# Two-layer S5 and gated DeltaNet step: Toeplitz products of the state space stage split into high and low parts

## The chip, the cores and the metric

The kernel runs on one core of one Trainium2 chip. The metric is the device time of one execution in microseconds (us), as the median of the runs. A core has five engines that run side by side and wait for each other by semaphores: TensorE (PE, matrix products), VectorE (DVE), ScalarE (ACT), GpSimd (POOL) and SyncE (SP, which only issues DMAs here). In this kernel products are written to tiles in PSUM, the other tiles lie in SBUF.

## The reference

Layer 0 is a diagonal complex state space mixer (S5), layer 1 a gated delta rule; both get 2048 prompt tokens and 8 samples of 16 tokens. Cut to what matters here:

```python
def s5_scan(u, h_re, h_im, ar, ai, bbr, bbi, c_re, c_im):
    # per position: x_t = Abar x_{t-1} + Bbar u_t, y_t = Re(C x_t); 64 groups, 16 channels, 64 states each
    ...

def s5_branch(h, ...):
    u, z = split(h @ w_in)
    y, hr, hi = s5_scan(u, ...)
    y = gelu(y + d * u)
    y = y * sigmoid(y @ w_glu + b_glu)
    y = y * silu(z)
    return y @ w_out, hr, hi
```

All arithmetic is float32.

## The kernel before

The program goes through stages: the S5 input products (to about 270 us of the profile), the state space stage (about 270 to 600 us), the gate and output products of layer 0, then layer 1. The change lies in the state space stage.

The tokens are cut into chunks of 8 (NCH = 272 chunks, 256 of them of the prompt). Within a chunk the recurrence is written as a Toeplitz matrix: the part of y that comes from the same chunk is one product of `toe` (128x128, 8 positions by 16 channels, from the impulse response with `d` on its diagonal) with `u` (128 x 272). What comes from earlier chunks goes over the states: `pb` is the chunk's contribution to the state (products of `ab` and `u`), VectorE rotates it by the tables `tw` (f, then z), scans along the chunks (`tensor_tensor_scan`), rotates back (t, then xs), and a product with `ca` adds it to y.

The stage has 16 blocks of 4 groups. `s5_setup(b)` makes `ab`, `ca` and the Toeplitz matrix of block b: the impulse response `kp` goes to DRAM (`k_d`) and comes back as `toe` in four DMAs. `s5_load(b)` loads u and tw. `s5_main(b)` does the block. The loop calls load and setup of block b+1 ahead of the main part of block b.

In most of its products the kernel writes a value as the sum of a high and a low part in the type `F32R`, and the product as three: high x high, high x low, low x high. A product of `F32R` stands as one record in the profile (one pass). `split_w` makes the parts: ScalarE casts the high part, VectorE (or the engine in `lo_eng`) subtracts for the low part. Before, `ca` and `xs` are split so, and `toe` x `u` is a float32 product.

Pools give each tile a number of buffers: b1 has one of each tag, b2 two. A tile's buffer is free when its readers are done. `ps_b` has one buffer for pb, `ps_y` two for py.

`z_block` is work of another kind: the z half of the input projection (tiles pdz, 64 blocks of 24 one-pass products of 128x272). Nothing in the stage waits for it. 58 of the blocks may run at any time, and fill PE; the last six are held until the last y products of the stage (`later([ends...])`).

What sets the order of instructions in this stage is a scheduler that works at build time with its own idea of durations; each engine then runs its list in order, and so a change of a few instructions moves the z products and others among them. When the stage is done, `ps5.close()` frees the SBUF of its pools, and the gate weights (wgr) are loaded there.

Of the kernel before, what the change touches and what calls it, by code (L numbers as in the profile page):

```python
# [11 lines left out]
F32R = mybir.dt.float32r  # L12
# [6 lines left out]
P = 128  # L19
# [3 lines left out]
NCH = 272  # L23
# [18 lines left out]
def bc(ap, axis, n):  # L42
    a = ap.unsqueeze(axis)
    shape = list(a.shape)
    shape[axis] = n
    return a.broadcast_to(shape)


def dram_ap(t, offset, dims):
    return bass.AP(t.tensor, t.offset + offset, [list(d) for d in dims])  # L50
# [3 lines left out]
def kernel(ctx: ExitStack, tc: tile.TileContext, I, O, upto="Z"):  # L54
    nc = tc.nc
# [18 lines left out]
    T, V, S, G, SY = (Engine(e) for e in (nc.tensor, nc.vector, nc.scalar, nc.gpsimd, nc.sync))  # L74
# [54 lines left out]
    def split_w(dst_hi, dst_lo, raw, lo_eng=None):  # L129
        S.copy(dst_hi, raw)  # L130
        (lo_eng or V).tensor_sub(dst_lo, raw, dst_hi.bitcast(F32))
# [102 lines left out]
    with ExitStack() as pa:  # L234
# [333 lines left out]
        for j in range(8):  # L568
            hh, hl = hcur
# [62 lines left out]
    with ExitStack() as pb:  # L632
        ps5 = pb.enter_context(ExitStack())
        b2 = ps5.enter_context(tc.tile_pool(reuse_waits="tile", name="b2", bufs=2))
        b1 = ps5.enter_context(tc.tile_pool(reuse_waits="tile", name="b1", bufs=1))
# [25 lines left out]
        def s5_setup(b):  # L661
            sp = b3.tile([P, SPW], F32, tag="sp", bufs=2, name=f"sp_{b}")
            nc.sync.dma_start(sp, sp_d[b])
            pw = sp[:, PWO:BBO].rearrange("p (l r n) -> p l r n", l=2, r=3)
            bbv = sp[:, BBO:BDO].rearrange("p (r l c) -> p r l c", r=2, l=2)
            bdv = sp[:, BDO:CCO].rearrange("p (r l m) -> p r l m", r=2, l=2)
            ccv = sp[:, CCO:SPW].rearrange("p (r l c) -> p r l c", r=2, l=2)

            abt = b1.tile([P, 2, 2, 8, 16], F32, tag="abt", name=f"abt{b}")
            tt = b1.tile([P, 2, 2, 9, 16], F32, tag="tt", name=f"abtt{b}")  # L670
            for l in range(2):
                V.tensor_mul(abt[:, l], bc(bc(bbv[:, 0, l], 1, 8), 1, 2), bc(pw[:, l, 0:2, 0:8], 3, 16))
                V.tensor_mul(tt[:, l, :, 0:8], bc(bc(bbv[:, 1, l], 1, 8), 1, 2), bc(pw[:, l, 1:3, 0:8], 3, 16))
            V.tensor_add(abt.rearrange("p l r n c -> p (l r) (n c)"), abt.rearrange("p l r n c -> p (l r) (n c)"),
                         tt.rearrange("p l r n c -> p (l r) (n c)")[:, :, 0:128])
            ab = b2.tile([P, 4, P], F32, tag="ab", name=f"ab{b}")
            pt = ps_t.tile([P, 4, P], F32, tag="t", name=f"abT{b}")
            for q in range(4):
                T.transpose(pt[:, q, :], abt[:, q // 2, q % 2].rearrange("p n c -> p (n c)"), ident)
            S.copy(ab, pt)  # L680

            ca = b3.tile([P, 2, 2, 9, 16], F32, tag="ca", bufs=2, name=f"ca{b}")
            t2 = b1.tile([P, 2, 2, 9, 16], F32, tag="tt", name=f"cat{b}")
            for l in range(2):
                V.tensor_mul(ca[:, l], bc(bc(ccv[:, 0, l], 1, 9), 1, 2), bc(pw[:, l, 1:3], 3, 16))
                V.tensor_mul(t2[:, l], bc(bc(ccv[:, 1, l], 1, 9), 1, 2), bc(pw[:, l, 0:2], 3, 16))
            V.tensor_sub(ca, ca, t2)
            cs_ = [b2.tile([P, 2, 2, P], F32R, tag="ca" + i, name=f"ca{i}{b}") for i in "hl"]
            split_w(*(t.rearrange("p l r (n c) -> p (l r) n c", c=16) for t in cs_),
                    ca[:, :, :, 1:9].rearrange("p l r n c -> p (l r) n c"))  # L690

            pk = ps_t.tile([P, P], F32, tag="t", name=f"pk{b}")
            for l in range(2):
                for r in range(2):
                    T.matmul(pk[32 * l:32 * l + 32, :], lhsT=bdv[:, r, l],
                             rhs=ca[:, l, r, 0:8, :].rearrange("p n c -> p (n c)"), start=(r == 0), stop=(r == 1),
                             tile_position=(0, 32 * l))
            kp = b2.tile([64, 240], F32, tag="kp", bufs=1, name=f"kp{b}")
            G.memset(kp[:, 0:112], 0.0)
            S.copy(kp[:, 112:240], pk[0:64])  # L700
            V.scalar_tensor_tensor(kp[:, 112:128], dmask, d16[:, b:b + 1], kp[:, 112:128], op0=ALU.mult, op1=ALU.add)
            nc.scalar.dma_start(k_d[b], kp)
            toe = b2.tile([P, 4, P], F32, tag="toe", name=f"toe{b}")
            for g in range(4):
                nc.sync.dma_start(toe[:, g, :], dram_ap(k_d[b], 16 * g * 240, [[16, 8], [240, 16], [1, P]]))
            return cs_, ab, toe

        def s5_load(b):
            u = b2.tile([P, 4, NCH], F32, tag="ur", name=f"u{b}")
# [6 lines left out]
        def s5_main(b, u, tw, ca, ab, toe):  # L716
            prs = slice(2 * b, 2 * b + 2)
            z = b2.tile([P, 2, 2, NPC], F32, tag="z", name="z")
            x = b2.tile([P, 2, 2, NCH], F32, tag="x", name=f"xs{b}")
            xh = x[:, :, :, NPC:NCH].rearrange("p l r (q h) -> p l r q h", h=2)  # L720
            G.memset(x[:, :, :, 0:1], 0.0)
# [5 lines left out]
            f = b2.tile([P, 2, 2, 2, NPC], F32, tag="f", name=f"f{b}")  # L727
            for pl in range(2):
                pb_ = ps_b.tile([P, 2, 512], F32, tag="b", name=f"pb{b}_{pl}")
                for ri in range(2):  # L730
                    for g2 in range(2):
                        T.matmul(pb_[64 * g2:64 * g2 + 64, ri, 0:NCH], lhsT=ab[:, 2 * pl + 1 - ri, 64 * g2:64 * g2 + 64],
                                 rhs=u[:, 2 * pl + g2], start=True, stop=True, tile_position=(0, 64 * g2))
# [34 lines left out]
            for pl in range(2):  # L768
                y = b2.tile([P, 2, NCH], F32, tag="y", name=f"y{b}_{pl}")
                pys = [ps_y.tile([P, NCH], F32, tag="y", name=f"py{b}_{2 * pl + i}") for i in range(2)]  # L770
                for i in range(2):
                    T.matmul(pys[i], lhsT=toe[:, 2 * pl + i], rhs=u[:, 2 * pl + i], start=True, stop=False)
                for r in range(2):
                    for wi, xi in ((0, 0), (0, 1), (1, 0)):
                        for i in range(2):
                            ln = slice(64 * i, 64 * i + 64)
                            i_ = T.matmul(pys[i], lhsT=ca[wi][ln, pl, r], rhs=xs[xi][ln, pl, r],
                                          start=False, stop=(r == 1 and wi == 1), tile_position=(64 * i, 0))
                ends.append(i_.ins)
                for i in range(2):  # L780
                    S.activation(y[:, i, :], pys[i], AF.Gelu_apprx_tanh)
                nc.scalar.dma_start(
                    dram_ap(y_d, (b // 2) * 8 * P * NCH + (4 * (b % 2) + 2 * pl) * NCH, [[8 * NCH, P], [1, 2 * NCH]]),
                    y.rearrange("p g c -> p (g c)"))
            return ends

        par = s5_setup(0)
        ld = s5_load(0)
        for b in range(16):
            nxt = (s5_load(b + 1), s5_setup(b + 1)) if b < 15 else None  # L790
            ends = s5_main(b, *ld, *par)
            if nxt:
                ld, par = nxt
# [501 lines left out]
    with pd:  # L1295
# [5 lines left out]
        def hcols(n0, n, s0=0):  # L1301

            g = sum(8 * q.stop <= n0 for q in CG)
            c = slice(n0 // 8 - CG[g].start, (n0 + n) // 8 - CG[g].start)
            return [[slots(h[i], g)[:, s0:, c] for h in hh_] for i in range(2)]
# [37 lines left out]
        for k in range(KC):  # L1343
            sh, xi = modT[:, 24 + k, 0:1], xa[:, k]
# [104 lines left out]
        with ExitStack() as pq:  # L1449
# [51 lines left out]
            for i0, (n0, n) in enumerate(NATT):  # L1501
                ps = psd1.tile([P, 512], F32, tag="d", name=f"pba{n0}")[0:32, 0:n]
                hh, hl = hcols(n0, n)
# [138 lines left out]
        for b in range(4):  # L1642
            rs, cs_ = slice(32 * b, 32 * b + 32), slice(32 * b, 32 * b + 32)
# [437 lines left out]
def _build(arrays, upto="Z"):  # L2081
    import concourse.bacc as bacc

    nc = bacc.Bacc("TRN2", target_bir_lowering=False, num_devices=1)
    I = {k: nc.dram_tensor("in_" + k, v.shape, F32, kind="ExternalInput").ap() for k, v in arrays.items()}
    O = {k: nc.dram_tensor("out_" + k, s, F32, kind="ExternalOutput").ap() for k, s in _OSHAPE.items()}
    with tile.TileContext(nc, schedule_with_timeline_sim=True) as tc:
        dbg = kernel(tc, I, O, upto)
    return nc, dbg
# [9 lines left out]
```

## Time and profile before

| | us |
|---|---|
| median of 3 runs | 2154.48 (2152.29 to 2161.67) |
| profiled execution: span from first to last instruction | 2147.2 |
| median less that span | 7.3 |
| PE busy | 2083.9 (97%) |
| DVE busy | 1558.8 (73%) |
| ACT busy | 980.2 (46%) |
| POOL busy | 473.6 (22%) |
| mean granted TensorE clock | 0.989 |

The profile is of one execution, in which the profiler recorded each instruction's start and end. Its page gives the span alone; the runs were timed apart from it, and the difference of 7.3 us is taken as what lies around a span. Busy time of an engine is the time in which it had an instruction under way; idle time that another engine ended is put down to that one ("<-"). Rows name the line of the kernel, the engine, the operation, the tile written and the tiles read. Each float32 product stands as two records.

### The profile page before, as it was taken

To read this page: it belongs to the slowest core of one execution; us is meant where nothing else is said; L and a number is where in the kernel's file an instruction comes from. 1 tells how busy PE (TensorE), PEld (TensorE's weight loads), DVE (VectorE), ACT (ScalarE), POOL (GpSimd) and SP (SyncE) were. 2 spreads that over 40 slices of the span, in tenths; PEclk is the share of its full clock that TensorE was granted. 3 is DMA by queue.
4 is the path that set the end of the run, shared out by engine and by line. 5 is a ranking of instruction groups with operands and counts; after the bars stand their busy time and mean duration, and the time that the engine had idled before them with its cause. 6 is when DMAs were issued, how large, how long until landed. Compare 5 with 4: busy or idle time off the path is not lost.

```text
span 2147.2 us, 42222 instructions
## 1 busy us (share of the span) xinstructions
PE 2083.9 (97%) x15729; PEld 1851.3 (86%) x15729; DVE 1558.8 (73%) x4017; ACT 980.2 (46%) x2298; POOL 473.6 (22%) x720
## 2 busy tenths in 40 slices
PE   6899999999799999999999999999999899999998
PEld 4888988888599999999888879889987688888887
DVE  6999498999756554446665669688556788888875
ACT  3543433333255544446665422341224556666663
POOL 1267310000112322222100000100011344444430
PEclk9999999999899999999999999999999999999999
DMA  9897744444386533336465313663456844444432
GB/s 278 273 299 234 239 150 149 141 157 148 97 242 220 190 113 110 108 100 218 138 202 171 92 50 86 162 146 103 135 169 217 269 143 126 134 142 147 147 113 70
DMA packets 398666, 344.99 MB, mean 161 GB/s; under 512 B 88410, under 2 KB 359274, under 8 KB 398460
## 3 DMA queue, kind: packets, MB, share of 16 engines
q1 hardware_dynamic: 261388, 234.95, 36.9%
q10 hardware_dynamic: 134256, 99.69, 14.4%
q0 software_dynamic: 2816, 7.65, 1.0%
q8 instruction: 124, 2.03, 0.4%
q14 instruction: 82, 0.67, 0.1%
HBM read 221.40 MB, written 120.80 MB: 159 GB/s over the span
## 4 chain that ended last, share of the span: by engine, by line
PE 86%; DVE 6%; DMA 4%; ACT 2%; issue 1%; SPq 1%; POOL 0%; ACTq 0%; DVEq 0%
PE epo L69 6%; PE pc L150 5%; PE pc L152 5%; PE pc L151 5%; PE pz L152 3%; PE po L150 3%; PE pz L151 3%; PE pdz L151 3%; PE pz L150 3%; PE po L152 3%; PE po L151 3%; PE pdz L150 3%; PE pdz L152 3%; PE pg L152 3%; PE pg L150 3%; PE pg L151 3%
## 5 line engine op out<-in xcount | busy, mean ns | idle before, releaser
L150 PE MATMUL pc<-h1h,wdh 128*128 128x512 f32 (+1 forms) x600 | 216.5, 361 | 0.0
L152 PE MATMUL pc<-h1h,wdl 128*128 128x384 f32 (+1 forms) x600 | 214.9, 358 | 0.0
L151 PE MATMUL pc<-h1l,wdh 128*128 128x384 f32 (+1 forms) x600 | 214.8, 358 | 0.1
L1414 DVE SCALAR_TENSOR_TENSOR ac<-pb,convw,ac 128x384 f32<-128x384 f32 (+3 forms) x288 | 163.6, 591 | 3.3
L150 PE MATMUL pdz<-hhz,wzh 128*128 128x272 f32 x512 | 152.3, 298 | 1.8 <-ACT evz L627 1.8
L151 PE MATMUL pdz<-hlz,wzh 128*128 128x272 f32 x512 | 153.0, 299 | 0.0
L152 PE MATMUL pdz<-hhz,wzl 128*128 128x272 f32 x512 | 151.6, 296 | 0.0
L150 PE MATMUL po<-gh,woh 128*128 128x272 f32 x512 | 148.6, 292 | 2.2 <-ACT gh L942 2.2
L151 PE MATMUL po<-gl,woh 128*128 128x272 f32 x512 | 148.4, 291 | 0.8 <-DVE gl L942 0.8
L152 PE MATMUL po<-gh,wol 128*128 128x272 f32 x512 | 148.7, 292 | 0.0
L151 PE MATMUL pg<-yl,wgh 128*128 128x272 f32 x512 | 148.4, 290 | 0.0
L150 PE MATMUL pg<-yh,wgh 128*128 128x272 f32 x512 | 147.5, 288 | 0.5 <-ACT evz L627 0.5
L152 PE MATMUL pg<-yh,wgl 128*128 128x272 f32 x512 | 147.5, 288 | 0.0
L150 PEld LDWEIGHTS pc<-h1h,wdh 128*128 128x128 f32 x600 | 112.6, 188 | 12.3 <-issue 1.7
L151 PEld LDWEIGHTS pc<-h1l,wdh 128*128 128x128 f32 x600 | 112.7, 188 | 10.4 <-issue 0.8
L152 PEld LDWEIGHTS pc<-h1h,wdl 128*128 128x128 f32 x600 | 112.6, 188 | 10.2 <-issue 0.8
L150 PE MATMUL pd<-hh,wuh 128*128 128x272 f32 x384 | 112.5, 294 | 0.0
L69 PE MATMUL epo<-w2h,ohi 128*128 128x512 f32 x272 | 111.7, 410 | 0.0
L152 PE MATMUL pd<-hh,wul 128*128 128x272 f32 x384 | 110.9, 289 | 0.0
L151 PE MATMUL pd<-hl,wuh 128*128 128x272 f32 x384 | 110.6, 288 | 0.0
L69 PE MATMUL epo<-w2l,ohi 128*128 128x512 f32 x272 | 107.5, 395 | 1.6 <-DMA w2l<-w2l_d 1.5
L939 POOL TENSOR_TENSOR zt<-zt,sz 128x272 f32<-128x272 f32 x64 | 63.4, 996 | 203.5 <-ACT sz L938 194.3
(613 smaller groups left out, 6373.7 us busy)
## 6 DMA issues: line engine op xcount, KB each, us to landing
wa<-in_w_ada SPq DMA_DIRECT2D x32, 512.0 KB
wdr<-in_w_in SPq DMA_DIRECT2D x24, 512.0 KB
h_d<-x ACTq DMA_DIRECT2D x8, 1088.0 KB
u_d<-ev ACTq DMA_DIRECT2D x64, 136.0 KB
hz<-h_d SPq DMA_DIRECT2D x16, 544.0 KB
u<-u_d SPq DMA_DIRECT2D x16, 544.0 KB
z_d<-evz ACTq DMA_DIRECT2D x64, 136.0 KB
y_d<-y ACTq DMA_DIRECT2D x32, 272.0 KB
```

The lines of the kernel that those rows point to most:

```text
L69: i_ = f(*a, **kw)
L150: T.matmul(ps, lhsT=w_hi[k], rhs=x_hi[k], start=(k == 0), stop=False)
L151: T.matmul(ps, lhsT=w_hi[k], rhs=x_lo[k], start=False, stop=False)
L152: i_ = T.matmul(ps, lhsT=w_lo[k], rhs=x_hi[k], start=False, stop=(k == n - 1))
L939: G.tensor_mul(zt, zt, sz)
L1414: V.scalar_tensor_tensor(o, src(j), convw[:, b, j:j + 1], o, op0=ALU.mult, op1=ALU.add)
```

## The change

In each block, `toe` and `u` are split into high and low parts (tiles toeh, toel, uh, ul, one buffer each); ScalarE casts the high parts, GpSimd subtracts for the low ones. The Toeplitz product is three one-pass products that start the sum in py. The split of `toe` stands in `s5_setup`, that of `u` in `s5_main`. The unsplit u is still read by the pb products. The part of SBUF set apart for GpSimd's DMA descriptors is 4096 bytes of each partition where it was 16384, and the four new tiles take 12800 bytes of each.

```diff
             for g in range(4):
                 nc.sync.dma_start(toe[:, g, :], dram_ap(k_d[b], 16 * g * 240, [[16, 8], [240, 16], [1, P]]))
-            return cs_, ab, toe
+            ths = [b1.tile([P, 4, P], F32R, tag="toe" + i, name=f"toe{i}{b}") for i in "hl"]
+            split_w(*ths, toe, G)
+            return cs_, ab, ths
...
         def s5_main(b, u, tw, ca, ab, toe):
             prs = slice(2 * b, 2 * b + 2)
             z = b2.tile([P, 2, 2, NPC], F32, tag="z", name="z")
+            us = [b1.tile([P, 4, NCH], F32R, tag="ur" + i, name=f"u{i}{b}") for i in "hl"]
+            split_w(*us, u, G)
...
                 for i in range(2):
-                    T.matmul(pys[i], lhsT=toe[:, 2 * pl + i], rhs=u[:, 2 * pl + i], start=True, stop=False)
+                    for wi, xi in ((0, 0), (0, 1), (1, 0)):
+                        T.matmul(pys[i], lhsT=toe[wi][:, 2 * pl + i], rhs=us[xi][:, 2 * pl + i],
+                                 start=(wi + xi == 0), stop=False)
...
-    nc = bacc.Bacc("TRN2", target_bir_lowering=False, num_devices=1)
+    nc = bacc.Bacc("TRN2", target_bir_lowering=False, num_devices=1, dynamic_dma_scratch_size=4096)
```

The order on three engines, around one block in the middle of the stage (block 5, counted from 0). The numbers behind the names are the buffers' running numbers and differ between the two programs; below, before stands first, then after. On TensorE, right behind the last products of the block's first two y tiles (py_0, py_1) with the low parts of its states:

```order
L777 MATMUL py_0_4930<-xsh_4925,cal_4729 128x272
L777 MATMUL py_1_4931<-xsh_4925,cal_4729 128x272
L151 MATMUL pdz_4_7123<-hlz_0_6822,wzh_4034 128x272
L152 MATMUL pdz_4_7123<-hhz_0_6821,wzl_4035 128x272
L150 MATMUL pdz_4_7123<-hhz_0_6821,wzh_4034 128x272
L151 MATMUL pdz_4_7123<-hlz_0_6822,wzh_4034 128x272
L152 MATMUL pdz_4_7123<-hhz_0_6821,wzl_4035 128x272
L150 MATMUL pdz_4_7123<-hhz_0_6821,wzh_4034 128x272
L732 MATMUL pb_1_5029<-u_4835,ab_4848 64x272 x4
```

```order
L783 MATMUL py_0_5022<-xsh_5017,cal_4797 128x272
L783 MATMUL py_1_5023<-xsh_5017,cal_4797 128x272
L736 MATMUL pb_0_5278<-u_5069,ab_5082 64x272 x4
L151 MATMUL pdz_3_7351<-hlz_0_7078,wzh_4036 128x272
L695 MATMUL pk_5250<-ca_5239,sp_5223 32x128 x4
```

Before, pb_1 of the next block (6) stands there, behind six z products, and the f that reads it stands a few instructions behind xsl of block 5 on VectorE's list. After, the place has pb_0 of block 7, and both pb of block 6 stand further ahead.

On ScalarE, between the GELUs of the block's first and second pair of y tiles:

```order
L781 ACTIVATE y_0_4929<-py_1_4931 128x272
L782 DMA y_d<-y_0_4929 128x544
L735 COPY bs<-pb_1_5029 128x32
L680 COPY ab_5116<-abT_5117 128x512
L130 CAST cah_4996<-ca_4989 128x512
```

```order
L787 ACTIVATE y_0_5021<-py_1_5023 128x272
L788 DMA y_d<-y_0_5021 128x544
L739 COPY bs<-pb_0_5278 128x32
L700 COPY kp_5255<-pk_5250 64x128
L702 DMA k_d_143<-kp_5255 64x240
L130 CAST toeh_4965<-toe_4960 128x512
L130 CAST uh_5120<-u_4919 128x1088
L130 CAST cah_5096<-ca_5089 128x512
L787 ACTIVATE y_1_5045<-py_2_5046 128x272
```

The two new casts are those of block 6; they stand ahead of cah and of the GELU of py_2, and write buffers that the Toeplitz passes into py_2 and py_3 of block 5 read.

On GpSimd, the same place, where before only small fills stood:

```order
L721 MEMSET xs_4882 128x4
L699 MEMSET kp_5005 64x112
L721 MEMSET xs_5016 128x4
L699 MEMSET kp_5139 64x112
L721 MEMSET xs_5150 128x4
```

```order
L725 MEMSET xs_5274 128x4
L131 TENSOR_TENSOR toel_4966<-toe_4960,toeh_4965 128x512
L699 MEMSET kp_5405 64x112
L131 TENSOR_TENSOR ul_5121<-u_4919,uh_5120 128x1088
L725 MEMSET xs_5424 128x4
```

Two subtractions per block came in, both reading SBUF twice.

## The prediction, made before the changed kernel ran

> **What bounds the kernel now.** I read the page first, then the stage that the change touches: the windows over it, the waits of VectorE, the chain of waits across its end, and the groups and the timeline of the engines that the change loads.
>
> ```profile
> span 2147.2 us, 42222 instructions
> PE 2083.9 (97%) x15729; PEld 1851.3 (86%) x15729; DVE 1558.8 (73%) x4017; ACT 980.2 (46%) x2298; POOL 473.6 (22%) x720
> ```
>
> The page shows TensorE (PE) busy for 97% of the span and GpSimd (POOL) for 22%. Shares of the whole say little about one stage, so the next view is the stretch of the state space stage, from VectorE's (DVE's) first f (280.8 us) to its last product of the stage (585.7 us).
>
> ```profile
> core 0: us, PE busy (x) PEld busy (x) DVE busy (x) ACT busy (x) POOL busy (x), PEclk, DMA share, GB/s
> 280.80:560.00 279.20, 279.20 (x2149) 232.75 (x2148) 253.61 (x539) 96.18 (x236) 4.31 (x29) 1.00 0.47 144
> 560.00:585.70 25.70, 15.31 (x75) 9.81 (x73) 25.13 (x46) 4.63 (x13) 8.32 (x8) 0.70 0.20 70
> ```
>
> Two engines are full here. Up to 560 us PE never rests, because the z products fill every hole; VectorE is busy for 253.61 of 279.20 us. Then the z products that may run ahead are used up, PE falls to 15.31 of 25.70 us at a granted clock of 0.70, and VectorE, which now hardly waits, is at 98%. In all VectorE works 278.7 us of 304.9 and rests 26.2. What it rests for:
>
> ```profile
> L737 DVE TENSOR_TENSOR f<-pb,tw 128x512 f32<-128x512 f32 x60 | 38.7, 681 | 20.2 <-ACT bs L735 20.2
> L131 DVE TENSOR_TENSOR cal<-ca,cah 128x512 fp32r<-128x512 f32 x14 | 9.6, 683 | 0.5 <-ACT cah L130 0.5
> ```
>
> 20.2 us of the 26.2 stand ahead of f, which needs the product pb (bs is the copy from the same product, just ahead of it): PE comes to pb late, behind z products. The chain of waits tells what ends the stage:
>
> ```profile
> 571.27 1.20 DVE xsl L131
> 572.47 1.70 DVE z L739
> 575.20 2.97 DVE z L746 x4
> 581.74 2.37 DVE t L760 x2
> 585.66 0.34 SPq L796
> 586.05 4.61 DMA wgr<-in_w_glu
> L150 PE MATMUL pg<-yh,wgh x512: 284/288/396, 616.2 to 987.3; 128*128 128x272 f32 x171
> ```
>
> The end is VectorE's: its last pieces lead at 585.7 us to the close of the stage's pools, then to the gate weights. PE has the last y products and six z blocks left and begins the gate products (pg) at 616.2 us. All that is unchanged behind the stage, so whatever shifts VectorE's end at 585.7 us shifts the rest by about as much.
>
> **The change part by part.** *PE.* 64 fp32 Toeplitz products go, and 192 of one pass come (64 products, three passes each).
>
> ```profile
> 368.13 1.08 PE L772 MATMUL py<-u,toe 128*128 128x272 f32 x4
> 369.14 0.39 PE L777 MATMUL py<-xsh,cah 64*128 64x272 f32 x2
> 376.22 0.29 PE L150 MATMUL pdz<-hhz,wzh 128*128 128x272 f32 x1
> 381.22 0.28 PE L151 MATMUL pdz<-hlz,wzh 128*128 128x272 f32 x1
> ```
>
> The first row is two fp32 products (two records each); the next instruction starts 1.01 us later, so one costs 0.505 us. The z rows are the first and last of 41 one-pass products of the same shape, 5.00 us for 40 steps, so 0.125 us each. That is 64 x 0.505 = 32.3 us out and 192 x 0.125 = 24.0 in: PE needs 8.3 us less, some 286 of the 294.5 us that it was busy in the stretch.
>
> *ScalarE (ACT).* It gains a high part of toe (128x512) and of u (128x1088) for each of 16 blocks.
>
> ```profile
> L130 ACT CAST xsh<-xs 128x1088 fp32r<-128x1088 f32 x14 | 15.4, 1100 | 15.7 <-DVE xs L763 13.5 <-DMA z_d<-evz 2.2
> L130 ACT CAST cah<-ca 128x512 fp32r<-128x512 f32 x13 | 8.1, 620 | 32.9 <-PE py L777 29.3 <-DMA k_d<-kp 3.6
> ```
>
> 16 x (1.10 + 0.62) = 27.5 us on an engine that works 96 of 279 us, so there is room. The new tiles have one buffer each, so both casts wait for the Toeplitz passes of the block before; queued behind them stand cah, the two GELUs and an evacuation evz, and VectorE's cal waits for cah. In the row cah itself rests 29.3 us for the last products of py, which come after those Toeplitz passes on PE, so most of the 1.72 us per block falls into that rest. Cost between 0 and 16 x 1.72 = 27.5 us; I take 0, as cal's own row shows a wait of only 0.5 us.
>
> *GpSimd.* It gains the two low parts per block. The nearest rows are its subtractions of the same kind, and a third row shows what VectorE does meanwhile:
>
> ```profile
> L1858 POOL TENSOR_TENSOR Sl<-Sf,Sh x28: 1277/1307/1320, 1719.4 to 2091.3; 128x512 fp32r<-128x512 f32 x28
> L1109 POOL TENSOR_TENSOR ekl<-ekq,ekh x14: 2369/2398/2436, 1714.0 to 2080.0; 128x1024 fp32r<-128x1024 f32 x14
> L1916 DVE SCALAR_TENSOR_TENSOR exo<-exo,es,fB x17: 1283/1285/3384, 1714.1 to 2142.4; 128x1024 f32<-128x1024 f32 x17
> L1871 DVE TENSOR_TENSOR oo<-oo,poc x30: 675/680/684, 1719.5 to 2116.6; 128x512 f32<-128x512 f32 x30
> ```
>
> 128x512 takes 1.31 us and 128x1024 takes 2.40; by the line through both, 128x1088 takes 2.53. So 3.84 us per block and 61.5 us for 16, on an engine that is almost idle here. By itself that is hidden. But the third row has one exo of 3384 ns among others of 1285: it started at 1714.1 us beside the first ekl (1714.0), and lasted until that had ended, 2.10 us longer. VectorE with two inputs in SBUF stands still while GpSimd reads SBUF. The fourth row, whose input poc is in PSUM, never does (675 to 684). The state space stage shows the same once, where GpSimd advances the sample states (timeline of POOL, then groups of VectorE within 570 to 581 us and within 280.8 to 560):
>
> ```profile
> 571.41 2.20 POOL L797 TENSOR_TENSOR ax<-ax,bs 128x512 f32<-128x512 f32 x1 [18.89 <-DVE xs L738]
> 578.76 1.29 POOL L799 TENSOR_TENSOR stN<-stN,bs 128x512 f32<-128x512 f32 x1
> L746 DVE TENSOR_TENSOR_SCAN z<-rN,z 128x128 f32<-128x128 f32 x4 | 3.0, 817 | 0.0
> L739 DVE TENSOR_TENSOR z<-f 128x512 f32<-128x512 f32 x1 | 1.8, 1784 | 0.0
> L752 DVE TENSOR_TENSOR cy<-cy 128x2 f32<-128x2 f32 x1 | 1.3, 1255 | 0.0
> L740 DVE TENSOR_TENSOR z<-f 128x512 f32<-128x512 f32 x1 | 1.1, 1105 | 0.0
> ...
> L746 DVE TENSOR_TENSOR_SCAN z<-rN,z 128x128 f32<-128x128 f32 x56 | 19.4, 403 | 0.0
> L739 DVE TENSOR_TENSOR z<-f 128x512 f32<-128x512 f32 x15 | 10.4, 691 | 0.0
> L740 DVE TENSOR_TENSOR z<-f 128x512 f32<-128x512 f32 x14 | 9.6, 684 | 0.0
> L752 DVE TENSOR_TENSOR cy<-cy 128x2 f32<-128x2 f32 x14 | 2.2, 158 | 0.3
> ```
>
> Beside eight GpSimd instructions (8.32 us by the window) VectorE lost 4 x 0.414 + 1.093 + 1.097 + 0.421 = 4.3 us, a share of 0.51, though part of those 8.32 us is GpSimd's own waiting. The exo lost 2.10 of 2.40, a share of 0.88. The new low parts are long, nearer to ekl, and they follow the Toeplitz passes of py_3, which follow xsl and the f of pb_1: VectorE is then at z and the scans, the very instructions that were held. Some will still meet an f, which reads PSUM and isn't held (38.7 of VectorE's 253.6 us). I take 0.8: 0.8 x 61.5 = 49 us on VectorE. Ends: 0.51 gives 31 us, 1.0 gives 61.5.
>
> The Trainium skill has this as a rule (SBUF — State Buffer, section "Who interferes with whom"): a VectorE instruction with two SBUF inputs contends with a GpSimd instruction that reads SBUF, and the loser blocks for the whole instruction. The trace agrees in kind; by that rule the loss would be all 61.5 us instead of 49, and the time 12 us longer than the sum below.
>
> *What the moved instructions give back.* The new order sets pb_0 and pb_1 of a block a full block ahead of the f that reads them (they stood just ahead of it), and u comes free at its split instead of after the Toeplitz products; SyncE's queue stood 83.6 us for that:
>
> ```profile
> SPq L710 <- PE py L772: 83.6, 13, 12.7
> ```
>
> So VectorE's rest for f goes: I let it fall to the 2.2% that the second window shows, 6.7 us of 304.9, a gain of 19.5 us (nothing at the low end, 26.2 at the high end). The z products spread to the end of the stage, which changes what PE waits for, not VectorE's work.
>
> *The DMA scratch.* It touches only DMAs that GpSimd issues:
>
> ```profile
> out_gdns<-s POOLq DMA_DIRECT2D x8, 512.0 KB, 4.5
> sp_d<-sp POOLq DMA_DIRECT2D x16, 155.0 KB, 4.3
> ```
>
> Cost 0, hidden in GpSimd's idle time. If each had to wait until the last one landed, GpSimd would stand 8 x 4.5 + 16 x 4.3 = 105 us, nearly all of it off the chain of waits; I allow 5 us. New DMAs there are none.
>
> *The sum.* VectorE's stretch: 278.7 of work + 49 of standing + 6.7 of rest = 334.4 us instead of 304.9, or +29.5; PE's 286 us fit beside it. What is late next is PE: in every block it waits for VectorE at pb or py, some (334 - 286)/16 = 3.0 us. The span goes from 2147.2 to about 2177 us. The median of the runs, 2154.48 us, lies 7.3 above the span; carried along, 2184 us. The ends are 31 - 26.2 = +5 (2159 us) and +61.5 (2216 us).
>
> **The rivals.** *VectorE isn't held, and it is faster.* Then VectorE needs 278.7 + 6.7 = 285.4 us and PE 286, both 19 us less than 304.9: 2135 us. For it speaks that GpSimd is idle and PE's products get cheaper; against it, the exo and the scans above. The point where it decides is a share of 19.5 / 61.5 = 0.32: below it, the change gains.
>
> *Held, but given back.* A share of 0.32 to 0.49 (up to 30 us lost) against the 19.5 gained ends within 0.5%, which is 10.8 us and about what a measurement of this kernel can tell from no change. It needs low parts that fall mostly on f or on rest. For it speaks the lower share, 0.51, of the eight short instructions; against it the length of the new ones and their place beside z and the scans.
>
> *Held, and PE slows too.* PE's waits of 3.0 us per block can bring the granted clock down.
>
> ```profile
> 610.95 0.53 PE L150 MATMUL pdz<-hhz,wzh 128*128 128x272 f32 x1 [1.78 <-ACT evz L627]
> 611.72 0.43 PE L150 MATMUL pdz<-hhz,wzh 128*128 128x272 f32 x1
> 614.59 0.29 PE L151 MATMUL pdz<-hlz,wzh 128*128 128x272 f32 x1
> ```
>
> After a gap of 1.78 us the products took 0.43 instead of 0.29 us for some 3.5 us, spaced 0.23 instead of 0.125, which loses 1.6 us. Once per block that is 26 us, of which PE's slack eats some; if half reaches VectorE, +13. With up to half of ACT's 27.5 us before cah, +14 more: 2197 to 2211 us, say 2205. The Trainium skill (TensorE: Matmul & The Clock Gate, section "HAM oscillation — how this bites in real kernels") puts the limit at idle gaps of about 3.4 us, by which 3.0 us would not throttle; the row above, at 1.78 us, speaks against so high a limit, and the measurement decides.
>
> **How the numbers follow.** Held and slower by about 30 us: 0.58. Held with a slow PE or a late cah, about 2205 us: 0.17. Held but given back: 0.14. Not held, 2135 us: 0.11. Slower is 0.75, same 0.14, faster 0.11. The likeliest case alone spans 2168 to 2198 us (shares of 0.6 to 0.95, and a few us of rest either way). The range reaches from 2152 us (inside the case that is given back) to 2212 us; outside it stay the faster case and the worst of the slow ones.
>
> **What would show it.** Right: t, scans and z of VectorE with single instructions up to 2.5 us longer than their least time, f unchanged, VectorE's busy time in the stage some 328 us, its wait for bs gone, and PE waiting on VectorE at pb or py in each block; gate products beginning near 646 us. GpSimd's toel near 1.3 and ul near 2.5 us when alone. The forecast is wrong if VectorE's durations stay as they are, if the wait for bs remains, or if cal comes to wait for cah in each block.

## The result, and the profile after

| | us |
|---|---|
| before (median of 4 runs) | 2153.39 (2152.27 to 2161.67) |
| after (median of 4 runs) | 2179.94 (2172.35 to 2184.00) |
| ratio after / before | 1.0113, 95% interval 1.0087 to 1.0139 |

The changed kernel is 1.1% slower, against a forecast of 2184 us in a range of 2152 to 2212. Its profiled execution has a span of 2182.3 us and took 2184.0 us.

The page of the changed kernel, the two lines whose counterparts stand first in the prediction:

```profile
span 2182.3 us, 42440 instructions
PE 2086.0 (96%) x15793; PEld 1860.2 (85%) x15793; DVE 1601.7 (73%) x4017; ACT 1002.3 (46%) x2330; POOL 562.0 (26%) x752
```

VectorE issues the same 4017 instructions as before and is busy for 42.9 us longer (1558.8 before). It got no new work, so the same instructions take longer. Where: the stretch from VectorE's first f to the end of its last xs, first in the kernel before, then in the changed one. The columns are those of the windows in the prediction: length, then busy time of PE, PE's weight loads, VectorE, ScalarE and GpSimd, then granted clock, DMA share and GB/s.

```profile
280.80:585.42 304.62, 294.51 (x2222) 242.56 (x2220) 278.53 (x583) 100.62 (x248) 12.63 (x37) 0.97 0.45 138
```

```profile
286.90:618.80 331.90, 297.20 (x2260) 249.10 (x2258) 320.69 (x583) 121.34 (x279) 86.22 (x68) 0.97 0.41 126
```

The stretch grew by 27.3 us. In it VectorE is busy 42.2 us longer, with 583 instructions in both, and rests 11.2 us instead of 26.1. GpSimd grew by 73.6 us. Which of VectorE's instructions grew, by its groups from 260 to 640 us, before and then after:

```profile
L760 DVE TENSOR_TENSOR t<-z,tw 128x1024 f32<-128x1024 f32 x32 | 37.7, 1217 | 0.2
...
L746 DVE TENSOR_TENSOR_SCAN z<-rN,cy,z 128x128 f32<-128x128 f32 x64 | 26.4, 466 | 0.0
...
L672 DVE TENSOR_TENSOR abt<-sp 128x256 f32<-128x256 f32 x32 | 12.3, 414 | 0.5 <-PE abT L679 0.5
```

```profile
L764 DVE TENSOR_TENSOR t<-z,tw 128x1024 f32<-128x1024 f32 x32 | 56.6, 1809 | 0.3
L741 DVE TENSOR_TENSOR f<-pb,tw 128x512 f32<-128x512 f32 x64 | 41.1, 681 | 2.4 <-ACT bs L739 2.4
L750 DVE TENSOR_TENSOR_SCAN z<-rN,cy,z 128x128 f32<-128x128 f32 x64 | 40.8, 699 | 0.0
...
L672 DVE TENSOR_TENSOR abt<-sp 128x256 f32<-128x256 f32 x32 | 15.6, 523 | 0.0
...
L131 DVE TENSOR_TENSOR cal<-ca,cah 128x512 fp32r<-128x512 f32 x16 | 11.4, 715 | 0.5 <-ACT cah L130 0.5
```

t grew by 18.9 us and the scans with cy by 14.4; f, whose input pb lies in PSUM, kept its 681 ns. The answers for single tiles give the least, median and longest duration in ns, first of t on VectorE, before and after, then of ul and of toel on GpSimd:

```profile
L760 DVE TENSOR_TENSOR t<-z,tw x32: 1207/1218/1226, 296.4 to 582.9; 128x1024 f32<-128x1024 f32 x32
```

```profile
L764 DVE TENSOR_TENSOR t<-z,tw x32: 1211/1224/3559, 305.0 to 616.3; 128x1024 f32<-128x1024 f32 x32
```

```profile
L131 POOL TENSOR_TENSOR ul<-u,uh x16: 2605/3019/4966, 279.7 to 611.4; 128x1088 fp32r<-128x1088 f32 x16
```

```profile
L131 POOL TENSOR_TENSOR toel<-toe,toeh x16: 1287/1304/3323, 294.3 to 610.2; 128x512 fp32r<-128x512 f32 x16
```

The median t is nearly unchanged (1218 and 1224 ns), but the longest lasted 1226 ns before and lasts 3559 after. GpSimd's own instructions stretch too, from 2605 to 4966 ns for ul. Two of PE's largest waits in the stage (us in total, times, longest), and the first pass of the gate products:

```profile
PE pb L736 <- DVE f L741: 20.2, 10, 3.5
...
PE py L777 <- POOL ul L131: 5.1, 3, 1.9
```

```profile
L150 PE MATMUL pg<-yh,wgh x512: 284/288/489, 649.3 to 1024.1; 128*128 128x272 f32 x171
```

The span grew by 35.1 us, more than the 26.6 us between the medians: every run whose span is on record took 1.7 to 1.8 us more than it, so the profiled execution of before must have taken some 2149 us, less than its four timed runs, while that of after is the longest of its four. The 35.1 us can be cut at these points. Until the first f: +6.1. The stretch: +27.3. From its end to the first gate product: 30.5 instead of 30.8 us, -0.3. Behind that: +2.0.

The 6.1 us ahead have two pieces, seen in VectorE's timeline, one row before, then two rows after:

```profile
276.38 0.74 DVE L672 TENSOR_TENSOR abt<-sp 128x256 f32<-128x256 f32 x2
```

```profile
264.51 1.23 DVE L138 TENSOR_TENSOR wzl<-wr,wzh 128x1024 fp32r<-128x1024 f32 x1 [4.00 <-ACT wzh L136]
...
280.16 3.06 DVE L672 TENSOR_TENSOR abt<-sp 128x256 f32<-128x256 f32 x2
```

The wait of 4.00 us for a weight of the stage before doesn't come from the new work: the kernel with three buffers of u (below), which has none of it, waits 4.07 us at the same place, and the one with filled low tiles doesn't. Whether the order makes it, or the single execution that was profiled, isn't shown. The two abt now start 3.8 us later and run beside GpSimd's first ul (from 279.65 us, 2.95 long): 2.3 us of standing.

### The profile page after: what moved, and what is told of

It reads as the page before. It is cut to its first block, busy times and chain, and to the rows that moved or that the text cites. A ratio compares the mean times of both kernels' runs of the same rounds, so it can differ in the third digit from the quotient of the medians.

```text
span 2182.3 us, 42440 instructions
## 1 busy us (share of the span) xinstructions
PE 2086.0 (96%) x15793; PEld 1860.2 (85%) x15793; DVE 1601.7 (73%) x4017; ACT 1002.3 (46%) x2330; POOL 562.0 (26%) x752
## 4 chain that ended last, share of the span: by engine, by line
PE 66%; DVE 18%; DMA 7%; issue 4%; ACT 2%; POOL 2%; SPq 1%; ACTq 0%; DVEq 0%; POOLq 0%
PE epo L69 7%; PE pc L150 5%; PE pc L152 5%; PE pc L151 5%; PE pz L152 3%; PE pz L151 3%; PE pz L150 3%; PE po L150 3%; PE po L151 2%; PE po L152 2%; DVE z L750 2%; PE pg L152 2%; PE pg L150 2%; PE pg L151 2%; PE epx L69 2%
## 5 line engine op out<-in xcount | busy, mean ns | idle before, releaser
L152 PE MATMUL pc<-h1h,wdl 128*128 128x512 f32 (+1 forms) x600 | 214.9, 358 | 0.0
L151 PE MATMUL pc<-h1l,wdh 128*128 128x512 f32 (+1 forms) x600 | 214.4, 357 | 0.0
```

The lines of the kernel that those rows point to most:

```text
L151: T.matmul(ps, lhsT=w_hi[k], rhs=x_lo[k], start=False, stop=False)
L152: i_ = T.matmul(ps, lhsT=w_lo[k], rhs=x_hi[k], start=False, stop=(k == n - 1))
```

## The experiments

The theory: VectorE's instructions with two inputs in SBUF stand while GpSimd reads SBUF for the low parts, and VectorE sets the end of the stage. The rivals put the loss on something else that came along: ScalarE's casts and the single buffers, the three passes with their new waits, the order, or the smaller DMA scratch.

### Both low parts on VectorE

```diff
-            split_w(*ths, toe, G)
+            split_w(*ths, toe)
-            split_w(*us, u, G)
+            split_w(*us, u)
```

> The changed kernel with both low parts on VectorE instead of GpSimd; nothing else is altered. If GpSimd's reading holds VectorE up (some 50 us in the stage), that goes, and VectorE gets the subtractions as work instead: by cal (0.68 us for 128x512) and xsl (1.2 us for 128x1088) about 1.9 us per block, 30 us for 16. About 20 us faster than the changed kernel: 2160 us, and still slower than the kernel before; t back at 1.2 us, scans at 0.40 us. If the 27 us come from ScalarE's casts, the single buffers, the order or the scratch instead, VectorE only gains work: 2180 to 2210 us.

Measured: 2155.57 us (the profiled execution took 2162.59); ratio to before 1.0012, interval 0.9994 to 1.0030. The page, groups of VectorE in the stage, and its stretch:

```profile
PE 2081.8 (96%) x15793; PEld 1857.6 (86%) x15793; DVE 1587.4 (73%) x4049; ACT 1005.5 (47%) x2330; POOL 482.7 (22%) x720
```

```profile
L764 DVE TENSOR_TENSOR t<-z,tw 128x1024 f32<-128x1024 f32 x32 | 37.7, 1218 | 0.3
...
L131 DVE TENSOR_TENSOR ul<-u,uh 128x1088 fp32r<-128x1088 f32 x16 | 20.5, 1280 | 0.0
```

```profile
288.40:598.24 309.84, 295.18 (x2282) 250.31 (x2281) 301.79 (x613) 124.42 (x281) 12.69 (x37) 0.96 0.44 135
```

t is back at 1218 ns. Doing the work itself costs VectorE less here than standing beside GpSimd: over the whole span it is busy 28.6 us longer than before, with 32 more instructions, against 42.9 with none; in the stretch 301.8 us instead of 320.7. The casts, the single buffers, the three passes and the scratch are all still there, so they don't make the 27 us. The time came out 4 us under the expectation, at the level of the kernel before rather than above it.

### The low tiles filled by GpSimd instead of subtracted

```diff
-            split_w(*ths, toe, G)
+            S.copy(ths[0], toe)
+            G.memset(ths[1].bitcast(F32), 0.0)
```

and the same for u.

> The changed kernel with the casts and all three passes, but GpSimd fills the low tiles with zeros instead of subtracting, so the low parts are left out of the products. GpSimd then writes SBUF and reads none. If it is GpSimd's reading that holds VectorE, VectorE's t and scans return to 1.2 and 0.40 us, and the stage needs about 285 us: 2135 to 2145 us, faster than both kernels. If writing holds it as well, a part stays, 2150 to 2170 us. If the casts, the single buffers, the order or the scratch cost the time, it stays near 2180 us.

Measured: 2137.01 us; ratio 0.9927, interval 0.9901 to 0.9953. GpSimd's fill of ul, VectorE's t, and the stretch:

```profile
L724 POOL MEMSET ul<- 128x1088 f32 x15 | 15.1, 1007 | 65.5 <-PE py L779 65.5
```

```profile
L766 DVE TENSOR_TENSOR t<-z,tw 128x1024 f32<-128x1024 f32 x32 | 37.7, 1220 | 0.3
```

```profile
281.30:570.57 289.27, 284.77 (x2286) 243.44 (x2284) 276.44 (x583) 123.63 (x279) 34.43 (x67) 1.00 0.47 145
```

GpSimd works 34.4 us in the stretch and VectorE loses nothing (276.4 us against 278.5 before). So GpSimd's fills, which write SBUF and read none of it, don't hold it here. The stretch is 15 us shorter than before, and this is the first rival of the prediction ("VectorE isn't held", 2135 us) with its condition met: once the standing is taken away, a gain is left. How much of it is due to the cheaper products isn't shown by this run; the last experiment comes within 3 us of its time with the float32 products.

### Each subtraction twice

```diff
             split_w(*ths, toe, G)
+            G.tensor_sub(ths[1], toe, ths[0].bitcast(F32))
             split_w(*us, u, G)
+            G.tensor_sub(us[1], u, us[0].bitcast(F32))
```

> The changed kernel with each of GpSimd's subtractions done twice in a row (same result). If VectorE is held while GpSimd reads, VectorE, which now rests only some 11 us in the stage, loses about 0.8 x 61.5 = 49 us more: about 2229 us, with GpSimd's share of the stage near 150 us. If GpSimd's time is off the path, and the loss comes from the casts, the order or the buffers, it stays within 5 us of 2180 us.

Measured: 2224.43 us; ratio 1.0325, interval 1.0294 to 1.0357. The stretch, and two groups of VectorE:

```profile
289.60:649.88 360.28, 299.44 (x2235) 252.89 (x2234) 355.74 (x583) 118.44 (x276) 147.62 (x95) 0.92 0.38 115
```

```profile
L766 DVE TENSOR_TENSOR t<-z,tw 128x1024 f32<-128x1024 f32 x32 | 55.1, 1763 | 0.5
...
L131 DVE TENSOR_TENSOR cal<-ca,cah 128x512 fp32r<-128x512 f32 x16 | 25.7, 1606 | 1.1 <-ACT cah L130 1.1
```

44.5 us more than the changed kernel, where 49 was expected. VectorE's busy time grew by another 35.1 us in the stretch, not by 49, and it has 4.5 us of rest left there. t lost no more than with one subtraction; the second one fell on other instructions, cal among them (1606 ns instead of 715). The mean granted clock fell to 0.92 here, with PE idle for 60.8 us of the stretch. The stretch itself is 28.4 us longer than in the changed kernel. Another 8.2 us lie behind it: the gate products start at 688.6 us, 38.7 us behind VectorE's last xs instead of 30.5, and in between the last Toeplitz products wait for GpSimd's last four subtractions, which run one behind the other from 653.4 to 660.8 us. So at the end of the stage GpSimd's time is on the path itself, and that the total came near 49 us is in part luck.

### The DMA scratch alone

```diff
-    nc = bacc.Bacc("TRN2", target_bir_lowering=False, num_devices=1)
+    nc = bacc.Bacc("TRN2", target_bir_lowering=False, num_devices=1, dynamic_dma_scratch_size=4096)
```

on the kernel before.

> The kernel before with the DMA scratch of 4096 bytes alone. By the prediction it costs nothing: within 2 us of the kernel before. If GpSimd's DMA issues wait for room in a smaller scratch, 2 to 10 us slower, which would explain the few us that the changed kernel lost outside the stage.

Measured: 2153.46 us; ratio 0.9994, interval 0.9979 to 1.0008. The scratch costs nothing.

### Float32 products, low parts made but unread

```diff
-            return cs_, ab, ths
+            return cs_, ab, toe
...
-                    for wi, xi in ((0, 0), (0, 1), (1, 0)):
-                        T.matmul(pys[i], lhsT=toe[wi][:, 2 * pl + i], rhs=us[xi][:, 2 * pl + i],
-                                 start=(wi + xi == 0), stop=False)
+                    T.matmul(pys[i], lhsT=toe[:, 2 * pl + i], rhs=u[:, 2 * pl + i], start=True, stop=False)
```

on the changed kernel.

> The changed kernel with the float32 Toeplitz products of before; the casts and GpSimd's subtractions still run, but nothing reads what they write. If GpSimd's reading is the whole cost, VectorE's t and scans stay as long as in the changed kernel and the time stays near it, 2175 to 2190 us (PE's work is 8 us more, but lies beside VectorE's). If the three passes, with their waits for the low parts, make the loss, it falls back to the kernel before, 2150 to 2160 us.

Measured: 2181.68 us; ratio 1.0116, interval 1.0093 to 1.0140. The stretch, and two groups of VectorE:

```profile
290.70:620.92 330.22, 302.02 (x2188) 245.46 (x2188) 317.60 (x583) 121.01 (x278) 87.75 (x67) 0.95 0.41 127
```

```profile
L764 DVE TENSOR_TENSOR t<-z,tw 128x1024 f32<-128x1024 f32 x32 | 41.0, 1320 | 0.2
...
L673 DVE TENSOR_TENSOR abtt<-sp 128x256 f32<-128x256 f32 x32 | 24.0, 784 | 1.4 <-DMA sp<-sp_d 1.3
```

With none of the new products, the whole loss is there: VectorE's 317.6 us is 39.1 above before. I had expected t to stay as long as after the change, and that was wrong: t lost little (1320 ns), and abtt nearly doubled (784 ns, where the kernels without GpSimd's reading have about 440). Which instruction stands changed with the order, and the sum hardly did (39.1 us here, 42.2 in the changed kernel).

### GpSimd reading one input instead of two

```diff
-            split_w(*ths, toe, G)
+            S.copy(ths[0], toe)
+            G.tensor_scalar_mul(ths[1], toe, 0.0)
```

and the same for u.

> As the kernel with filled low tiles (the low parts are left out of the products, they are zeros), but GpSimd makes the zeros by reading toe and u and multiplying by zero: one SBUF input instead of two, and the same writes. If any reading of SBUF by GpSimd holds VectorE, t is longer than its 1.22 us, and the time stands between the filled tiles (2137 us) and the changed kernel (2180 us): by half the reading about 2158 us. If only two inputs contend, it is 2137 us, and if the held time goes by instructions and not by what they read, 2170 to 2180 us.

Measured: 2143.77 us (the profiled execution took 2151.61); ratio 0.9953, interval 0.9937 to 0.9969. The stretch, VectorE's t, and GpSimd's reading of u:

```profile
289.40:586.59 297.19, 287.59 (x2278) 243.88 (x2276) 291.95 (x584) 122.17 (x279) 88.32 (x68) 0.99 0.46 141
```

```profile
L766 DVE TENSOR_TENSOR t<-z,tw 128x1024 f32<-128x1024 f32 x32 | 42.2, 1358 | 0.4
```

```profile
L724 POOL TENSOR_SCALAR ul<-u 128x1088 fp32r<-128x1088 f32 x16 | 51.9, 3241 | 51.7 <-issue 33.2 <-PE py L779 18.5
```

GpSimd is busy for 88.3 us in the stretch, as with the subtractions (86.2), but VectorE's busy time is 13.4 us above before, not 42.2. So the loss doesn't go by how long GpSimd's instruction lasts. With one input instead of two it was about a third. That fits a loss that goes by what GpSimd reads, but the multiplication is also another instruction than the subtraction, and no run tells the two apart. The time lies nearer to the filled tiles than the 2158 us of my middle case.

### The kernel before with three buffers of u

```diff
-            u = b2.tile([P, 4, NCH], F32, tag="ur", name=f"u{b}")
+            u = b2.tile([P, 4, NCH], F32, tag="ur", bufs=3, name=f"u{b}")
```

with the scratch of 4096 bytes, on the kernel before.

> The kernel before with u in three buffers, for which the smaller scratch (which by itself changed nothing) makes room; products and engines as before, float32 Toeplitz products included. SyncE's queue no longer waits for the Toeplitz products to free u, so pb can run earlier. If the rest that VectorE takes for pb, 20 us, comes from that wait, most of it goes: 2140 to 2146 us, bounded by PE's 294.5 us against the stage's 304.9. If the rest comes from where pb stands in the order on PE, or from the one PSUM buffer of pb, nothing changes: 2150 to 2155 us.

Measured: 2139.95 us (2136.79 to 2143.98); ratio to before 0.9925, interval 0.9904 to 0.9947. VectorE's wait for f, the stretch, and what SyncE now waits for:

```profile
L737 DVE TENSOR_TENSOR f<-pb,tw 128x512 f32<-128x512 f32 x64 | 41.0, 683 | 1.9 <-ACT bs L735 1.9
```

```profile
285.10:569.59 284.49, 282.10 (x2149) 232.70 (x2148) 275.54 (x583) 99.22 (x244) 11.80 (x37) 1.00 0.47 143
```

```profile
SPq L705 <- PE py L772: 66.5, 14, 11.0
```

The rest for f fell from 20.2 to 1.9 us, and SyncE waits for the Toeplitz products only to load the next toe (L705), no longer u. But the order changed too: in the traces, 21 of the 32 groups of pb products stand earlier on PE than before, most of them by twelve products into py, half a block. Whether the buffer alone would have done it, or only with the order that the scheduler made of it, isn't shown. This version beats both kernels: 0.7% under before and, by the two ratios, 1.9% under the changed one, with the float32 products left in place. I had called PE's 294.5 us a bound of the stretch; it was none. z products moved out of it, and PE's 282.1 us fit in 284.5. Of the 20.1 us that the stretch is shorter than before, 4.3 are lost ahead of it (the first f starts at 285.1 us) and 4.0 behind it (the gate products start 34.8 us after the last xs).

## Why the prediction was right, point by point

The mechanism and the sign were right, and the time is 4 us off. That it came so near is in part luck: several terms were off in opposite directions.

- **VectorE sets the end.** Right. The gate products came 33.1 us later, with VectorE's last xs 33.4 us later. The gate weights now start 10 us behind VectorE's end, as the chain shows (the last Toeplitz products come late and free the pools), yet the gate products keep their distance of 30.5 us, so the gap shows no cost:

```profile
618.21 0.61 DVE xs L767
...
628.09 0.65 PE py L777 x5
...
629.29 5.43 DMA wgr<-in_w_glu
```

- **Standing beside GpSimd, 49 us.** Right in kind, 7 too many: 42.2 us in the stretch. With the 2.3 us beside the first ul, ahead of it, that is 44.5 us, a share of 0.72 of the 61.5 instead of 0.8. The lone durations were right (1.29 and 2.61 us at the least, against 1.31 and 2.53), as was the longest t, 2.35 us above its least. Part of what I put on VectorE alone fell on GpSimd, whose low parts took 77.1 us, 15.6 more than the 61.5. The rule that I quoted from the Trainium skill (SBUF — State Buffer, section "Who interferes with whom"), taken as a hold of VectorE for all of GpSimd's instruction, would have given 61.5; the runs show less with two inputs, and much less with one (13.4 us). The same section says that GpSimd's writing doesn't contend with an instruction of two inputs, and the filled tiles agree: 34.4 us of GpSimd, nothing lost.
- **Rest falls from 26.2 to 6.7 us.** Right in kind, 4.5 us too far: 11.2 us of rest stayed. The wait ahead of f went from 20.2 to 2.4 us, but the wait for pb isn't gone: the small xs behind f, which reads the copy bs of the same product, now waits 2.6 us, where it didn't before:

```profile
DVE xs L742 <- ACT bs L739: 2.6, 2, 1.8
```

  The prediction named two reasons for the gain, pb earlier in the order and u free earlier. The three buffers of u show that most of the rest goes without any splitting (9.0 us stayed); since the order moved with them, the two reasons aren't told apart.
- **PE, 8.3 us less, and ScalarE's casts, 0.** Both off the path, as predicted: the run with float32 products and casts takes the changed kernel's time within 2 us, and cal waits 0.5 us for cah as before. Over the whole span PE is busy 8.1 us longer in that run than in the changed kernel (2094.1 and 2086.0), so the price of the products was about right. The 286 us of PE in the stretch were not: it was busy for 297.2, with 2260 records of products where the stretch had 2222 before.
- **PE waits next, 3.0 us per block at pb or py.** In part. PE is idle for 34.7 us of the stretch, 2.2 per block; 20.2 of its waits are at pb, for f, but 10 times and not in every block. The rival of a slow clock came in part. The mean granted clock of the stretch is 0.97 in both kernels, but before, it was 1.00 up to 560 us and fell when the z products ran out; after, it dips in the middle of the stage. One window of each, before and then after:

```profile
560.00:580.00 20.00, 13.80 (x73) 9.31 (x71) 19.57 (x36) 4.24 (x11) 8.27 (x8) 0.75 0.22 77
```

```profile
340.00:360.00 20.00, 16.52 (x103) 12.47 (x101) 19.53 (x31) 6.83 (x16) 3.87 (x3) 0.83 0.36 101
```

  Within the stretch this can't have cost more than VectorE's 11.2 us of rest, 4.5 above the forecast. Neither limit for an idle gap fits all gaps of this run, the 3.4 us of the Trainium skill (TensorE: Matmul & The Clock Gate, section "HAM oscillation — how this bites in real kernels") or one below 1.78. PE stood for 1.84 us until 374.71, and the granted clock of the 3.7 us behind that was 0.54; it stood for 2.94 us until 434.22, and the clock behind that stayed at 1.00.
- **The scratch, 0.** Right, by its own run.
- **The sum.** The stretch was put at +29.5 us and grew by 27.3: 42.2 of standing less 14.9 of rest. Too much standing, by 6.8, met too large a gain in rest, by 4.6. Missing from the sum were the 6.1 us ahead of the first f. On the other side, I carried 7.3 us from the span to the median as if they lay around every span. Only 1.7 to 1.8 us do in any run on record, so the other 5.6 were the distance of before's profiled execution from its median, and that step was wrong. These two errors, of about 6 us each, cancelled by luck, and what is left is the profiled execution of after, 4 us above its own median. By the medians alone, 26.6 us were measured where 29.5 were forecast.

## What to carry to other kernels

Work given to an idle engine wasn't free here, because it read SBUF beside a full VectorE: subtracting on GpSimd cost VectorE 43 us, where subtracting on VectorE itself cost 29. Before giving work away, look for the two-input instructions of VectorE that it would run beside, and ask what the full engine still rests for. Here that was a product whose operand waited for a buffer; a third buffer, with the order that came with it, brought 0.7% of the whole time without touching the arithmetic.

## What was unexpected of the hardware

- The loss runs both ways. With the subtractions VectorE lost 42.2 us in the stretch and 2.3 ahead of it, and GpSimd's toel and ul took 77.1 us (26.0 and 51.1) where 61.5 were expected of them alone, 15.6 more: 60.1 in all. With the float32 products it is 39.1 us of VectorE in the stretch and 20.2 of GpSimd (81.7 instead of 61.5), 59.3 in all. So in both kernels the two losses add up to about the time that GpSimd's reading needs. With the subtractions doubled they add up to less, 77.2 and 27.9 us (150.9 instead of 123) against 123, of which 7.4 run behind VectorE's last xs. Why one engine stands in one place and the other in another was not tested.
- One input read by GpSimd's multiplication takes longer (ul 2964 ns at the least) than its two-input subtraction (2605 ns at the least), and still disturbs VectorE less. Why was not tried.
